# Separate buffers for the expert tables, and DMAs moved from SyncE's queue to ScalarE's and GpSimd's, in a two-layer attention, RWKV and PEER backbone

## The chip, the cores and the metric

The kernel runs on one core of a Trainium2 chip. The metric is the device time of one execution in microseconds, as a median over runs. The core's engines are TensorE (PE in the profile, with weight loads as PEld), VectorE (DVE), ScalarE (ACT), GpSimd (POOL) and SyncE (SP); SyncE computes nothing here and issues DMAs. Each engine works through its own instructions in a fixed order. A DMA is issued by one engine, in that order, and is then carried by the core's 16 DMA engines.

## The reference

Two layers work on 512 latent tokens and 256 context tokens of width 1024, in float32. Each layer has a mixer (windowed attention, 2-D neighbourhood attention and an RWKV-7 scan in parallel, one output projection) and then a PEER feed-forward part. The change touches PEER and the loads around it:

```python
def peer_ffn(h, wq, sub_keys, u, v):
    ...
        q = (hb @ wq).reshape(PEER_CHUNK, PEER_HEADS, 2, PEER_QDIM // 2)
        s = jnp.einsum('thpd,hpnd->thpn', q, sub_keys).astype(jnp.float32)
        sv, si = lax.top_k(s, PEER_TOPK)
    ...
        expert = i1 * PEER_NKEYS + i2
        gate = jax.nn.softmax(best, axis=-1)
        ue = jnp.take(u, expert, axis=0)
        ve = jnp.take(v, expert, axis=0)
        act = jax.nn.gelu(jnp.einsum('td,thkd->thk', hb, ue).astype(jnp.float32), approximate=False)
        return jnp.einsum('thk,thkd->td', (gate * act).astype(hb.dtype), ve)
```

Each token picks 16 of 16,384 experts in each of 8 heads, so 128 experts a token. An expert is one row of `u` (its score with the token goes through Gelu and is multiplied by the gate) and one row of `v` (which is added with that weight). In layer 0 all six tiles of 128 tokens pass through PEER; in layer 1 only the four latent ones are needed.

## The kernel before, in words

PEER is computed in two ways at once. Some token tiles are *dense*: four in layer 0, three in layer 1. For them TensorE multiplies the tokens with all 16,384 experts, and gates that are zero for experts not chosen pick out the right ones. The other tiles are *gathered*: the two context tiles in layer 0, one latent tile in layer 1. For them GpSimd issues indirect DMAs (`gather`, L1461) that fetch, for one of a token's 128 choices, the rows of `u` and `v` of 128 tokens: 128 rows of 8 KB, 1 MiB a gather. There are 256 gathers in layer 0 and 128 in layer 1. For each pair (`accumulate`) VectorE forms two dot products (L1472), ScalarE takes Gelu of both (L1474), VectorE multiplies by the gates (L1475) and adds the two `v` rows with these weights to `acc` (L1478).

A dense layer goes through its experts in 128 blocks of 128, four to a group, two to a table load of 1 MiB.

- Scores (`scored(g)`): a table `ur2` holds two blocks of `u` transposed (L1304). ScalarE rounds each to `uH` (L1311), VectorE takes the rest `uL` (L1313), and TensorE makes 24 matmuls into `pa` (three products, eight slices of the width), 512 columns wide in layer 0 and 384 in layer 1. ScalarE's Gelu gives `aw` (L1317), which is written to DRAM as `ascr` (L1319), or is kept in SBUF and multiplied by its gates at once. That is so for the last blocks: 32 in layer 0, 44 in layer 1. These read their gates back from DRAM as `wt`, one row buffer for a group (L1300): 8 reads in layer 0, 11 in layer 1. Hence 96 and 84 writes of `ascr`.
- Gates (`gates`): spread over the first groups (22 in layer 0, 18 in layer 1), one-hot matrices from VectorE and small matmuls into `pw` (L1233) make the gates of 32 tokens for all experts; ScalarE copies them to `W` (L1234, one buffer), and a 2 MiB DMA writes them to `wscr` (L1236): 16 writes in layer 0, 12 in layer 1.
- Values: with all scores done, a second loop loads tables of `v` (L1364), reads `ascr` and `wscr` back (L1357, L1359; none for kept blocks), rounds and splits (`vH`, `vL`, `GH`, `GL`), and accumulates in PSUM (`py`). Two blocks of layer 0 are 48 matmuls of 512 columns here too.

In layer 0's scores the modulation weights of layer 1 are also worked out: after every fifth group a `mod_unit` loads four row buffers of `w_mod` (L167), six units in all.

All these loads share one ring of row buffers (8 KB a partition): gathers, tables of both kinds, `wt`, `w_mod`, and, in the stages before, w_out, wq and residual rows. A buffer is given out in the order in which the program asks, so a request waits until the sixth request before it is done with:

```python
NROW = 6
NTICK = ((2, 1.2, 2.6, 1.75), (0, 0, 1.3, 0.9))
...
    def row(self):
        return self.gp.tile([P, 2 * D], F32, name="row", bufs=NROW)
```

How many gathers are asked for beside the dense work is set by `tick`. `NTICK[l][z]` is added to a count at each tick, and a gather is issued for each whole number. In layer 0: index 0, five ticks late in the latent `scores`; index 1, after every second block of the first 12 groups (24 ticks); index 2, the same in the other 20 groups (40 ticks); index 3, after every second block of the values (64 ticks). In layer 1 the first kind ends after 3 groups. What is left is gathered by `flush` after the values. Then `ends` and the lines after it multiply by the modulation, add the residual and write the result.

A scheduler fixes the order of the instructions on each engine when the program is built, by priorities and a simulated timeline; gathers and what belongs to them have a high priority. Before the change all the DMAs named here are in SyncE's queue, but for the gathers, which are in GpSimd's.

Of the kernel before, what the change touches and what calls it, by code (L numbers as in the profile page):

```python
# [18 lines left out]
P = 128  # L19
# [15 lines left out]
LATER = 2000  # L35
NROW = 6
NQ = 2
# [18 lines left out]

NTICK = ((2, 1.2, 2.6, 1.75), (0, 0, 1.3, 0.9))
NFIRST = (12, 3)
# [7 lines left out]
class Kernel:  # L66
# [82 lines left out]
    def mod_unit(self, l, ch, pool, ps, tag, row=None):  # L149
# [10 lines left out]
        for k in range(KC):  # L160
            if row is None:
                w = pool.tile([P, 1024], F32, name="wmod")
                nc.sync.dma_start(w, src[:, k])
            else:
                if k % 2 == 0:
                    w2 = row().rearrange("p (k n) -> p k n", k=2)
                    nc.sync.dma_start(w2, src[:, k:k + 2])  # L167
                w = w2[:, k % 2]
            for j in range(4):
                add(j, self.cs[:, k], w[:, j * 256:j * 256 + 256], k == 0, False)  # L170
# [1030 lines left out]
    def gates(self, t, pk, pool, ps):  # L1201
# [16 lines left out]
        for s_ in range(4):  # L1218
            W = pool.tile([P, P, 32], F32, name="W", bufs=1)
            for t4 in range(8):  # L1220
# [10 lines left out]
                for q in range(4):  # L1231
                    for z in range(2):
                        nc.tensor.matmul(pw[:, q], oh[:, 1, :, q], og[:, z, :, q], start=z == 0, stop=z == 1)  # L1233
                nc.scalar.activation(W[:, :, t4 * 4:t4 * 4 + 4], pw.rearrange("p q i -> p i q"), AF.Copy,  # L1234
                                     scale=1.0 / GSCALE)
            nc.sync.dma_start(self.wscr[:, 4 * t + s_], W)  # L1236
            yield
# [22 lines left out]
    def peer(self, l, st):  # L1260
# [11 lines left out]
        with ExitStack() as sb:  # L1272
# [23 lines left out]
            def scored(g, late=None):  # L1296

                if 4 * g >= P - nres - LATE[l]:
                    wt = gat.row()[:, :4 * nd].rearrange("p (a q t) -> p a q t", q=4, t=32)
                    nc.sync.dma_start(wt, self.wscr[:, :nd // 32, g * 4:g * 4 + 4, :])  # L1300
                for b in range(4 * g, 4 * g + 4):
                    if b % 2 == 0:
                        ur2 = gat.row().rearrange("p (z k n) -> p z k n", z=2, k=KC)
                        nc.sync.dma_start(ur2, i["uT"][l, b:b + 2].rearrange("z p k n -> p z k n"))  # L1304
# [13 lines left out]
                    if b not in keep:  # L1318
                        nc.sync.dma_start(self.ascr[g, :, b % 4, :nd], aw)  # L1319
                    else:  # L1320
# [26 lines left out]
        with ExitStack() as sb:  # L1347
# [5 lines left out]
            for g in list(range(n0, 32)) + list(range(n0)):  # L1353
# [6 lines left out]
                for q in range(4):  # L1360
                    b = g * 4 + q
                    if b % 2 == 0:
                        vr2 = gat.row().rearrange("p (z d) -> p z d", z=2)
                        nc.sync.dma_start(vr2, vtab[b * P:(b + 2) * P, :].rearrange("(z p) d -> p z d", p=P))  # L1364
# [64 lines left out]
class Gather:  # L1429
# [26 lines left out]
    def row(self):  # L1456
        return self.gp.tile([P, 2 * D], F32, name="row", bufs=NROW)

    def gather(self, a, k):
        r = self.row()  # L1460
# [6 lines left out]
    def accumulate(self, a, k):  # L1467
# [6 lines left out]
        nc.scalar.activation(dt, dt, AF.Gelu)  # L1474
        nc.vector.tensor_tensor(dt, dt, self.gate[:, a, k:k + NQ], OP.mult)  # L1475
        for z in range(NQ):
# [85 lines left out]
```

## Time and profile before

| what | value |
|---|---|
| median of 3 runs | 5024.15 us (5021.28 to 5025.62) |
| profiled execution, its own time | 5011.65 us |
| its span in the trace | 5009.9 us |
| TensorE busy | 4425.2 us, 88% of the span |
| VectorE busy | 3653.8 us, 73% |
| ScalarE busy | 1772.4 us, 35% |
| GpSimd busy | 1226.5 us, 24% |
| mean granted TensorE clock | 0.917 of full speed |
| bytes moved | 1186.55 MB, mean 237 GB/s |

The profile is one execution. An engine is busy while it runs an instruction; matmuls overlap, so TensorE's busy time doesn't say how fast it works, and the number of matmuls in a stretch is shown beside it. The granted clock is in parts of full speed (2.4 GHz; the lower level is 1.2 GHz), averaged over a stretch. The DMA share is the mean busy share of the 16 DMA engines.

### The profile page before, as it was taken

To read this page: it belongs to the slowest core of one execution; us is meant where nothing else is said; L and a number is where in the kernel's file an instruction comes from. 1 tells how busy PE (TensorE), PEld (TensorE's weight loads), DVE (VectorE), ACT (ScalarE), POOL (GpSimd) and SP (SyncE) were. 2 spreads that over 40 slices of the span, in tenths; PEclk is the share of its full clock that TensorE was granted. 3 is DMA by queue.
4 is the path that set the end of the run, shared out by engine and by line. 5 is a ranking of instruction groups with operands and counts; after the bars stand their busy time and mean duration, and the time that the engine had idled before them with its cause. 6 is when DMAs were issued, how large, how long until landed. Compare 5 with 4: busy or idle time off the path is not lost.

```text
span 5009.9 us, 74083 instructions
## 1 busy us (share of the span) xinstructions
PE 4425.2 (88%) x27525; PEld 3669.7 (73%) x27525; DVE 3653.8 (73%) x7587; ACT 1772.4 (35%) x2961; POOL 1226.5 (24%) x1347
## 2 busy tenths in 40 slices
PE   7778887789999988899999886799698997999999
PEld 4557776667787776677788664777588996988787
DVE  3974666889877876677788878557579875676776
ACT  3533245333333332222232354335334332333333
POOL 0025632151112222222222115354031110111120
PEclk9788797899999998999999987889899998999999
DMA  7444654255778888887999834573526885886897
GB/s 268 149 113 124 175 174 157 101 190 199 272 288 340 335 310 309 320 305 274 334 373 351 286 117 120 129 202 103 176 92 219 323 296 223 289 307 251 310 328 243
DMA packets 573481, 1186.55 MB, mean 237 GB/s; under 512 B 62768, under 2 KB 376000, under 8 KB 520384
## 3 DMA queue, kind: packets, MB, share of 16 engines
q1 hardware_dynamic: 506688, 758.39, 45.0%
q0 software_dynamic: 61440, 418.41, 22.6%
q10 hardware_dynamic: 4992, 5.02, 0.4%
q8 instruction: 216, 3.54, 0.3%
q14 instruction: 145, 1.19, 0.1%
HBM read 1005.19 MB, written 176.50 MB: 236 GB/s over the span
## 4 chain that ended last, share of the span: by engine, by line
PE 45%; DVE 16%; issue 15%; DMA 15%; POOL 4%; ACT 3%; SPq 1%; POOLq 0%; ACTq 0%; DVEq 0%
DMA row<-in_uv,eidx 6%; PE py L133 5%; PE py L132 4%; PE py L134 4%; PE pa L132 4%; PE pa L134 4%; PE pa L133 4%; PE pw L1233 3%; DMA row<-in_uT 3%; PE pf L132 2%; POOL row L1461 2%; PE pf L133 2%; PE pf L134 2%; DVE uL L1313 1%; PE pg L840 1%
## 5 line engine op out<-in xcount | busy, mean ns | idle before, releaser
L1461 POOL DMA_INDIRECT row<-in_uv,eidx x384 | 547.4, 1426 | 2350.1 <-DVE accc L1478 1153.0
L132 PE MATMUL pa<-hH,uH 128*128 128x512 f32 (+1 forms) x2048 | 772.8, 377 | 81.9 <-ACT uH L1311 68.0
L134 PE MATMUL pa<-hH,uL 128*128 128x512 f32 (+1 forms) x2048 | 764.6, 374 | 21.1 <-DVE uL L1313 21.0
L133 PE MATMUL pa<-hL,uH 128*128 128x512 f32 (+1 forms) x2048 | 762.8, 372 | 0.0
L133 PE MATMUL py<-vL,GH 128*128 128x512 f32 x1792 | 699.8, 392 | 19.8 <-DVE vL L1369 19.6
L134 PE MATMUL py<-vH,GL 128*128 128x512 f32 x1792 | 697.1, 391 | 0.0
L132 PE MATMUL py<-vH,GH 128*128 128x512 f32 x1792 | 684.3, 392 | 13.3 <-ACT vH L1367 9.2
L1472 DVE SCALAR_TENSOR_TENSOR row<-row,h2c 128x1024 f32<-128x1024 f32 x384 | 473.6, 1236 | 230.3 <-DMA row<-in_uv,eidx 229.8
L132 PEld LDWEIGHTS pa<-hH,uH 128*128 128x128 f32 x2048 | 399.5, 195 | 138.9 <-ACT uH L1311 79.0
L1478 DVE SCALAR_TENSOR_TENSOR accc<-row,dt,accc 128x1024 f32<-128x1024 f32 x384 | 494.2, 1287 | 5.7
L1311 ACT CAST uH<-row 128x1024 fp32r<-128x1024 f32 x256 | 266.2, 1049 | 570.1 <-PE pa L133 435.7
L134 PEld LDWEIGHTS pa<-hH,uL 128*128 128x128 f32 x2048 | 397.4, 194 | 74.6 <-DVE uL L1313 32.7
L1313 DVE TENSOR_TENSOR uL<-row,uH 128x1024 fp32r<-128x1024 f32 x256 | 311.6, 1222 | 161.4 <-ACT uH L1311 156.4
L133 PEld LDWEIGHTS pa<-hL,uH 128*128 128x128 f32 x2048 | 398.8, 195 | 40.1
L133 PEld LDWEIGHTS py<-vL,GH 128*128 128x128 f32 x1792 | 338.6, 189 | 97.2 <-DVE vL L1369 26.9
L132 PEld LDWEIGHTS py<-vH,GH 128*128 128x128 f32 x1792 | 339.2, 189 | 86.0 <-ACT vH L1367 10.0
L134 PEld LDWEIGHTS py<-vH,GL 128*128 128x128 f32 x1792 | 338.8, 189 | 70.0
L1369 DVE TENSOR_TENSOR vL<-row,vH 128x1024 fp32r<-128x1024 f32 x256 | 311.5, 1220 | 13.4 <-ACT vH L1367 13.1
L1367 ACT CAST vH<-row 128x1024 fp32r<-128x1024 f32 x256 | 266.4, 1044 | 15.5 <-DMA row<-in_uv 13.5
L1225 DVE TENSOR_TENSOR oh<-iota,ix 128x512 f16<-128x512 f16 x448 | 171.9, 421 | 135.5 <-PE pw L1233 135.1
L1233 PE MATMUL pw<-og,oh 128*128 128x128 f16 x1792 | 237.9, 297 | 36.4 <-DVE og L1228 19.2
L1233 PEld LDWEIGHTS <-oh 128*128 128x128 f16 x1792 | 190.4, 119 | 76.6 <-DVE og L1228 35.1
(380 smaller groups left out, 8352.1 us busy)
## 6 DMA issues: line engine op xcount, KB each, us to landing
row<-in_uT SPq DMA_DIRECT2D x128, 1024.0 KB
row<-in_uv SPq DMA_DIRECT2D x128, 1024.0 KB
wscr<-W SPq DMA_DIRECT2D x28, 2048.0 KB
wmod<-in_w_mod SPq DMA_DIRECT2D x48, 512.0 KB
row<-in_wq SPq DMA_DIRECT2D x24, 1024.0 KB
ascr<-aw SPq DMA_DIRECT2D x96, 256.0 KB
row<-in_w_mod SPq DMA_DIRECT2D x24, 1024.0 KB
av<-ascr SPq DMA_DIRECT2D x48, 512.0 KB
```

Of the source, the lines that this page charges most:

```text
L132: mm(out, lh, rh, start=first, stop=False)
L133: mm(out, lh, rl, start=False, stop=False)
L134: mm(out, ll, rh, start=False, stop=last)
L1225: nc.vector.tensor_tensor(oh[:, z], self.iota4, ix[:, z, tt].unsqueeze(1).to_broadcast([P, P, 4]), OP.is_equal)
L1233: nc.tensor.matmul(pw[:, q], oh[:, 1, :, q], og[:, z, :, q], start=z == 0, stop=z == 1)
L1311: nc.scalar.copy(uH, ur)
L1313: nc.vector.tensor_tensor(uL, ur, uH.bitcast(F32), OP.subtract)
L1367: nc.scalar.copy(vH, vr)
L1369: nc.vector.tensor_tensor(vL, vr, vH.bitcast(F32), OP.subtract)
L1461: self.K.nc.gpsimd.indirect_dma_start(out=r, out_offset=None, in_=self.K.i[f"uv{self.l}"], in_offset=bass.IndirectOffsetOnAxis(ap=self.idx ...
L1472: nc.vector.scalar_tensor_tensor(rows[z][:, 0:D], rows[z][:, 0:D], 1.0, self.h[:, a], OP.mult, OP.mult, accum_out=dt[:, z:z + 1])
L1478: nc.vector.scalar_tensor_tensor(acc, v, dt[:, z:z + 1], acc, OP.mult, OP.add)
```

## The change

- The tables of scores and values get a ring of their own of two buffers (`table`, `NTAB`); four are left for everything else.
- The writes of `ascr` and `wscr` are issued by ScalarE, the reads of `wt` and the loads of `w_mod` by GpSimd, in place of SyncE.
- In `accumulate`, the two products with the gates become two ScalarE operations with the gate as scale, in place of one on VectorE.
- The gather rates change: in layer 0 from 2.6 to 2.3 in the later scores and from 1.75 to 1.9 in the values, in layer 1 from 1.3 to 1.2 and from 0.9 to 1.0.

```diff
-NROW = 6
+NROW = 4
+NTAB = 2
...
-NTICK = ((2, 1.2, 2.6, 1.75), (0, 0, 1.3, 0.9))
+NTICK = ((2, 1.2, 2.3, 1.9), (0, 0, 1.2, 1.0))
...
                     w2 = row().rearrange("p (k n) -> p k n", k=2)
-                    nc.sync.dma_start(w2, src[:, k:k + 2])
+                    nc.gpsimd.dma_start(w2, src[:, k:k + 2])
...
-            nc.sync.dma_start(self.wscr[:, 4 * t + s_], W)
+            nc.scalar.dma_start(self.wscr[:, 4 * t + s_], W)
...
                     wt = gat.row()[:, :4 * nd].rearrange("p (a q t) -> p a q t", q=4, t=32)
-                    nc.sync.dma_start(wt, self.wscr[:, :nd // 32, g * 4:g * 4 + 4, :])
+                    nc.gpsimd.dma_start(wt, self.wscr[:, :nd // 32, g * 4:g * 4 + 4, :])
...
-                        ur2 = gat.row().rearrange("p (z k n) -> p z k n", z=2, k=KC)
+                        ur2 = gat.table().rearrange("p (z k n) -> p z k n", z=2, k=KC)
...
-                        nc.sync.dma_start(self.ascr[g, :, b % 4, :nd], aw)
+                        nc.scalar.dma_start(self.ascr[g, :, b % 4, :nd], aw)
...
-                        vr2 = gat.row().rearrange("p (z d) -> p z d", z=2)
+                        vr2 = gat.table().rearrange("p (z d) -> p z d", z=2)
...
+    def table(self):
+        return self.gp.tile([P, 2 * D], F32, name="tab", bufs=NTAB)
+
...
-        nc.vector.tensor_tensor(dt, dt, self.gate[:, a, k:k + NQ], OP.mult)
+        for z in range(NQ):
+            nc.scalar.activation(dt[:, z:z + 1], dt[:, z:z + 1], AF.Copy, scale=self.gate[:, a, k + z:k + z + 1])
```

## Rows read from the trace of the kernel before

**Rows 1.** Busy us (instructions) per engine in stretches, granted clock, DMA share, GB/s

```profile
1400.00:1500.00 100.00, 100.00 (x573) 81.40 (x572) 73.49 (x127) 34.24 (x57) 16.18 (x14) 1.00 0.82 311
...
1600.00:1700.00 100.00, 95.88 (x481) 78.13 (x479) 78.76 (x128) 31.66 (x55) 22.93 (x16) 0.95 0.89 341
...
1700.00:2140.00 440.00, 372.39 (x1829) 293.21 (x1830) 309.69 (x453) 116.28 (x189) 101.97 (x71) 0.92 0.87 319
...
2500.00:2600.00 100.00, 100.00 (x443) 82.80 (x442) 86.12 (x114) 29.78 (x45) 22.79 (x17) 1.00 1.01 376
...
4080.00:4460.00 380.00, 333.04 (x1910) 319.31 (x1909) 251.67 (x378) 121.28 (x195) 53.30 (x42) 0.91 0.74 270
4460.00:4860.00 400.00, 390.19 (x1709) 320.34 (x1708) 291.48 (x400) 144.22 (x216) 63.25 (x43) 1.00 0.85 298
```

**Rows 2.** TensorE's matmuls of tile `pa` alone, in stretches

```profile
1400.00:1500.00 100.00, 77.88 (x328) 1.00 0.82 311
1700.00:2140.00 440.00, 307.49 (x1248) 0.92 0.87 319
...
4080.00:4460.00 380.00, 295.56 (x1571) 0.91 0.74 270
4300.00:4400.00 100.00, 94.46 (x521) 0.97 0.81 298
```

**Rows 3.** TensorE's waits, 1700 to 2140 us: total us, times, longest

```profile
PE pa L132 <- ACT uH L1311: 40.7, 10, 11.7
PE pm L159 <- DMA row<-in_w_mod: 10.7, 5, 4.6
```

**Rows 4.** Timeline of ScalarE, 1895 to 1960 us

```profile
1926.76 1.99 ACT L1311 CAST uH<-row 128x1024 fp32r<-128x1024 f32 x2 [11.30 <-DMA row<-in_uT]
```

**Rows 5.** TensorE's waits, 4080 to 4460 us

```profile
PE pa L132 <- ACT uH L1311: 26.0, 5, 15.4
PE pw L1233 <- ACT W L1234: 8.1, 2, 7.0
...
PE pa L132 <- ACT aw L1317: 3.2, 2, 2.8
```

**Rows 6.** TensorE's waits, 3700 to 4080 us

```profile
PE pa L132 <- ACT aw L1317: 8.5, 7, 2.8
```

**Rows 7.** TensorE's waits, 2140 to 2400 us

```profile
PE py L132 <- ACT vH L1367: 9.2, 2, 6.7
```

**Rows 8.** SyncE's queue: waits, 1700 to 2140 us

```profile
SPq L1319 <- ACT aw L1317: 76.8, 17, 15.8
SPq L1304 <- DVE accc L1478: 55.4, 8, 12.0
```

**Rows 9.** Timeline of SyncE's queue, 1895 to 1960 us

```profile
1897.94 7.72 SPq L167 DMA_DIRECT2D row<-in_w_mod  x4
1906.61 0.55 SPq L1300 DMA_DIRECT2D row<-wscr  x1
1907.68 11.61 SPq L1304 DMA_DIRECT2D row<-in_uT  x2
```

**Rows 10.** VectorE's waits over the whole span

```profile
DVE row L1472 <- DMA row<-in_uv,eidx: 229.8, 91, 7.9
```

**Rows 11.** Instructions of L1319: ns min/median/max, first and last start

```profile
L1319 SPq DMA_DIRECT2D ascr<-aw x180: 319/320/1259, 1151.2 to 4213.0; - x180
```

**Rows 12.** Instructions of L502, a plain DMA in GpSimd's queue

```profile
L502 POOL DMA_DIRECT2D tscr<-tt x32: 764/772/817, 301.4 to 3244.8; - x32
```

**Rows 13.** Instructions of L1461, the gathers

```profile
L1461 POOL DMA_INDIRECT row<-in_uv,eidx x384: 932/1214/4301, 1017.6 to 4921.8; - x192
```

**Rows 14.** Groups by line: busy us, mean ns of one, idle before

```profile
L1474 ACT ACTIVATE dt<-dt 128x2 f32<-128x2 f32 x192 | 38.8, 202 | 479.2 <-DVE row L1472 479.0
...
L1475 DVE TENSOR_TENSOR dt<-dt,gatec 128x2 f32<-128x2 f32 x192 | 29.8, 155 | 15.0 <-ACT dt L1474 15.0
```

**Rows 15.** Timeline of VectorE at the end of layer 0, 2815 to 2880 us

```profile
2851.36 1.28 DVE L1478 SCALAR_TENSOR_TENSOR accc<-row,dt,accc 128x1024 f32<-128x1024 f32 x1
```

## The prediction

> **What bounds the kernel now.** I read the busy time by stretch first. The PEER part of layer 0 runs from about 1,150 to 2,870 us, that of layer 1 from about 3,560 us to the end; each is a stretch of scores (uT tables, matmul tile `pa`) and then one of values (uv tables, tile `py`). TensorE stands out in all of them, so the question is how much of each stretch it loses. Its pitch at full rate is seen in [rows 1]: in the values of layer 0, 443 matmuls filled 100 us, 0.2257 us each. In the scores, `pa` is mixed with gate matmuls [rows 1, 2]: of 573 matmuls in a fully busy 100 us, 328 are `pa`, 328 x 0.2257 = 74.0 us, which leaves 26 us for 245 others, 0.106 us each. The narrower `pa` of layer 1 took 94.46 / 521 = 0.181 us [rows 2].
>
> Now the two scoring stretches that fall behind. In 1700 to 2140 us TensorE issued 1829 matmuls, 1248 of them `pa` [rows 1, 2]: 1248 x 0.2257 + 581 x 0.106 = 343 us of work in 440 us, 97 us lost. Of these 440 - 372.4 = 67.6 us were idle; the other 29 us are matmuls at the lower of the clock's two levels (granted 0.92 there against 1.00 in the full slices), which follows the pauses. In 4080 to 4460 us it is 1571 x 0.181 + 339 x 0.106 = 321 us in 380 us: 59 lost, 47 idle, 12 slow. The values of layer 1 are at 390.2 of 400 us busy, and those of layer 0 reach 100 of 100: little is to be had there.
>
> What ended the idle time says which part is the tables' [rows 3 to 7]: in the first stretch 40.7 of 67.6 us are `uH`, ScalarE's rounding of a table, and ScalarE itself was waiting for the table to land (11.30 us in [rows 4]); 10.7 us are a w_mod row. In the second 26.0 us are `uH`, 8.1 us `W` and 3.2 us `aw`, the two tiles whose writes SyncE issues. Between 3700 and 4080 us `aw` costs another 8.5 us, and in 2140 to 2400 us a late value table 9.2 us.
>
> Why the tables are late stands in SyncE's own queue [rows 8, 9]. It waited 76.8 us at L1319 for an activation to write, and 55.4 us at L1304 for a gather's accumulation to free a shared buffer. Before the 11.30 us pause, four w_mod loads and a gate read went first, and only then the two tables, whose issues took 11.61 us together and which landed 19 us after 1907.68.
>
> **The change part by part.** *Own buffers for tables.* A table now waits only for the table two before it. A period is two blocks, 48 `pa` matmuls or 10.8 us at full rate; the old ring of six served one table, 2.6 gathers and about half a row of other loads in it, so it went round in 6 / 4.1 = 1.5 periods, and the tables' wait hung on gathers. Two periods, 21.7 us, stand against the 19 us landing that hurt. Gathers keep their depth: 4 / (2.3 + 0.5) = 1.4 periods in place of 1.5. In layer 0 the 40.7 us of idle time bring their share of slow clock, 40.7 / 67.6 x 97 = 58 us. The bytes limit this: 319 GB/s over 440 us are 140.4 MB; the 26 periods move 26 x 0.3 = 7.8 gathers of 1.05 MB away, which leaves 132.2 MB, 388 us at the 341 GB/s of [rows 1] (52 us gained) or 352 us at its 376 GB/s (88 us). From below, at the present 319 GB/s, 414 us: 26 gained. I take 40, three quarters of 52, since VectorE still waits for gathers in its own order (229.8 us over the run, [rows 10]) and a table is rounded there too.
>
> *Writes on ScalarE's queue.* 180 `ascr` and 28 `wscr` writes leave SyncE, which keeps almost nothing but tables while scoring. An issue took 0.320 us, at most 1.259 [rows 11]: 208 x 0.32 = 67 us of ScalarE's time, in stretches where it is about 30% busy (116.3 of 440 us). What waits behind one is the next rounding; the write's own wait is short, since ScalarE made the data just before. Cost 0, bound 10 us. A write held like the 11.61 us pair would hold a rounding, but in 180 none was held over 1.3 us. The return in layer 1, with `uH`, is (26.0 + 8.1 + 3.2) / 47 x 59 = 47 us; I take three quarters, 35, and 6 of the 8.5 us before it. Bytes don't limit here (270 GB/s).
>
> The Trainium skill says in "DMA: Bandwidth & Descriptors", under "Issuing engines are not separate DMA queues", that DMAs started by several engines run on the same 16 DMA engines, so that spreading them saves only the issuing time. By that rule the moved writes give nothing: a rival below. The trace speaks against it only so far as one queue's order makes a ready load wait behind an unready write: 76.8 us in [rows 8].
>
> *w_mod and gate reads on GpSimd's queue.* 24 w_mod loads (6 units of four) and 19 gate reads, 43 issues. A plain GpSimd issue took 0.77 us, a gather's 1.21 (up to 4.30) [rows 12, 13]: 33 to 52 us on an engine busy for 102 of the 440 us of the first stretch. Behind a waiting one stand the gathers, behind them VectorE. One w_mod unit takes all four row buffers. Both ends: nothing, as the gathers have 1.4 periods, or 7.9 us, the longest gather wait, for each of 6 units and 19 reads, 198 us. The mean of those waits is 229.8 / 91 = 2.5 us; I take 0 in the sum, as a ring of about equal depth leaves gathers where they were, and keep the other end as a rival.
>
> *Gate product on ScalarE.* Out go 192 VectorE products of 0.155 us, 30 us; in come 384 ScalarE ops. Nearest is the Gelu of the same tile, 0.202 us [rows 14]: 78 us. VectorE then waits some 0.3 us longer per pair, unless other work stands between. Neither engine is full. Cost 0, bounds -10 and +15.
>
> *New gather rates.* Layer 0: 40 ticks at 2.3 for 2.6 while scoring, 64 at 1.9 for 1.75 in the values: -12 and +9.6. Before, 254 of 256 gathers went out on ticks; now 252, and one more pair is flushed after the last tick. The last accumulation already ends the stage [rows 15]; four VectorE passes of some 1.25 us, 5 us more. In the values 1 table, 1.9 gathers and 1 MiB of reads a period are 4.09 MB, at 376 GB/s 10.88 us against TensorE's 10.84: 2 us in 48 periods (at 351 GB/s it would be 39). Against that stands 7 of the 9.2 us of the late value table. I put the values at 0, -7 to +32.
>
> *Four rows instead of six elsewhere.* w_out, wq and residual rows have less prefetch: 5 us, bounds 0 and 15, the trace showing no such wait.
>
> Sum: -40 - 35 - 6 + 0 + 5 + 5 = -71 us. The profiled execution took 5011.65 us (span 5009.9), 12.5 under the median of the runs: 5011.65 - 71 = 4941, so 4953 us by the runs' median, 1.4% less. A measurement tells about 0.2%, 10 us, from no change.
>
> **The rivals.** *All the lost time returns*: the pauses end altogether, and with them the slow clock. 97 + 59 + 8 - 10 = 154 us, 4870. For it: TensorE reaches 100 of 100 us where the tables are on time. Against: 132.2 MB then need 385 GB/s, more than any slice shows.
>
> *Moved queues are worth nothing* (the page's rule): `W` and `aw` stay late. The sum loses 11 us (three quarters of 11.3 / 47 x 59) and the 6: -54, 4970.
>
> *The wait passes from tables to gathers*: each engine's order is fixed at build time, and VectorE stands at a late gather with `uL` behind it. For it: those waits are 229.8 us today. A third more, 76 us, ends at 5024 or just above: no change.
>
> *GpSimd's queue makes it slower*: a gate read or a w_mod load waits at its head for a row, and gathers behind it come too late for VectorE's order. 25 such places at 5 us are 125 us: -71 + 125 = +54, 5078. It decides from 71 / 25 = 2.8 us a place, just above today's mean of 2.5. For it: the ring of four is filled by one w_mod unit. Against: the same loads took ring places before.
>
> The Trainium skill's "SBUF — State Buffer", under "SBUF: two separate sides", warns that descriptors of a GpSimd DMA can't be written while VectorE holds the shared port, and advises the queues of ScalarE or SyncE. The spread of the gather's issue, 0.93 to 4.30 us, agrees in direction; no run here separates it.
>
> **How the numbers follow.** The forecast, 4885 to 5000 around 4953, gets 0.48; all returned 0.14; queues worth nothing 0.08; passed to gathers 0.12; slower by GpSimd's queue 0.18. So faster 0.70, same 0.12, slower 0.18. The range 4860 to 5050 leaves out some 0.06 below and 0.13 above.
>
> **What would show it.** Right: the 40.7 and 26.0 us of `uH` fall to a third, granted clock in the two stretches above 0.95, scoring of layer 0 some 40 us shorter, the values unchanged. Wrong: VectorE's wait for gathers well over 230 us, GpSimd standing at L167 or L1300, or ScalarE standing at a write.

## The result, and the profile after

The changed kernel takes 4965.82 us (median of 4 runs, 4963.13 to 4971.35); the kernel before took 5022.72 us beside it (4 runs, 5010.22 to 5025.62). The ratio is 0.9893, 95% interval 0.9874 to 0.9912: 57 us or 1.1% faster. The forecast was 4953 us, 12.8 us below the result. The two profiled executions, 5011.65 and 4964.34 us, differ by 47.3, and the account below is made with them. So the time is close to the forecast; the parts that make it up are not, as the rest shows.

Lines of the changed kernel: score tables are loaded at L1305, rounded to `uH` at L1312; `aw` comes from L1318 and is written at L1320; `W` comes from L1235; gates are read at L1301; value tables are loaded at L1365 and rounded to `vH` at L1368; gathers are L1465, their dot products L1476, the gate product L1480, the accumulation L1483. The matmuls of `pa` and `py` are at L133 to L135.

Five landmarks on TensorE cut the run into stages. These are the rows of its matmuls by tile, for the kernel before (nanoseconds, then first and last start in us); the third is the value stage of layer 0 alone.

```profile
L134 PE MATMUL pa<-hH,uL x2048: 333/389/796, 1104.8 to 4463.7; 128*128 128x512 f32 x94, 128*128 128x384 f32 x93
L134 PE MATMUL py<-vH,GL x1792: 387/389/628, 2128.0 to 5001.5; 128*128 128x512 f32 x200
L132 PE MATMUL py<-vH,GH x1024: 387/389/795, 2124.2 to 2851.6; 128*128 128x512 f32 x171
L132 PE MATMUL py<-WH,oH x128: 389/393/794, 950.6 to 3608.3; 128*128 128x512 f32 x128
```

The same rows of the changed kernel:

```profile
L135 PE MATMUL pa<-hH,uL x2048: 331/389/687, 1020.0 to 4388.5; 128*128 128x512 f32 x94, 128*128 128x384 f32 x93
L135 PE MATMUL py<-vH,GL x1792: 387/389/628, 2054.8 to 4954.1; 128*128 128x512 f32 x200
L133 PE MATMUL py<-vH,GH x1024: 388/389/794, 2049.6 to 2781.5; 128*128 128x512 f32 x171
L133 PE MATMUL py<-WH,oH x128: 387/393/796, 932.5 to 3547.6; 128*128 128x512 f32 x128
```

Taking differences of these starts gives the time of each stage, in us:

| stage | before | after | difference |
|---|---|---|---|
| start to first value matmul of layer 0 | 2124.2 | 2049.6 | -74.6 |
| values of layer 0 | 727.4 | 731.9 | +4.5 |
| from there to the end of layer 1's output projection (left-over gathers, mixer) | 756.7 | 766.1 | +9.4 |
| scores of layer 1, to the last `pa` | 855.4 | 840.9 | -14.5 |
| values of layer 1, to the last `py` | 537.8 | 565.6 | +27.8 |
| all | 5001.5 | 4954.1 | -47.4 |

Two things are seen at once. The gain ahead of layer 0's values is nearly twice the 40 us forecast, and that of layer 1's scores about a third of the 41. And 28 us are lost again in a stage for which the forecast had nothing. How far a stage differs between kernels that share its code is seen below; layer 1's scores are the one where this matters.

TensorE's waits of the changed kernel over the whole span (total us, times, longest) no longer have a line for `uH`, which answers to [rows 3, 5]; what heads them is a value table, where [rows 7] had 9.2 us:

```profile
PE py L133 <- ACT vH L1368: 41.8, 26, 3.8
...
PE pa L133 <- ACT aw L1318: 22.7, 16, 2.6
PE pw L1234 <- ACT W L1235: 22.6, 8, 5.3
...
PE pa L133 <- ACT ar L1318: 15.2, 2, 7.7
```

From VectorE's waits over the span, which answer to [rows 10]: the wait for gathers has fallen from 229.8 to 73.0 us. (The longest is now that of `GL` for ScalarE's `GH`, 210.5 us, where it was 78.7.) The second line, a wait for gates read back, has no counterpart in the kernel before; it is taken up below.

```profile
...
DVE row L1476 <- DMA row<-in_uv,eidx: 73.0, 40, 7.1
DVE ar L1323 <- DMA row<-wscr: 59.6, 6, 23.3
```

The two scoring stretches that were read before in [rows 1], up to their ends (columns as there), and then TensorE's `pa` alone in them:

```profile
1700.00:2050.00 350.00, 309.63 (x1571) 248.74 (x1570) 233.48 (x335) 111.49 (x210) 81.87 (x62) 0.92 0.84 305
3960.00:4389.00 429.00, 391.11 (x2350) 377.00 (x2348) 278.78 (x423) 155.26 (x269) 63.13 (x46) 0.94 0.70 251
```

```profile
1700.00:2050.00 350.00, 262.08 (x1099) 0.92 0.84 305
3960.00:4389.00 429.00, 332.16 (x1816) 0.94 0.70 251
```

By the prediction's pitches the work in them is 1099 x 0.2257 + 472 x 0.106 = 298 us of 350, and 1816 x 0.181 + 534 x 0.106 = 385 of 429. So 52 and 44 us are still lost, where it was 97 of 440 and 59 of 380, and the granted clock is 0.92 and 0.94, not above 0.95. What ended the idle time that is left is spread over many things: in the first stretch 11.5 us for the first `GH` of the values, 7.7 for `ar`, 7.6 for `W` and 5.5 for a w_mod row; in the second 11.1 us for `W`, 9.4 for `uL` (VectorE's part of a table) and 7.5 for `ar`.

### The profile page after: what moved, and what is told of

Read it like the earlier page. It is cut to its first block, busy times and chain, and to the rows that moved or that the text cites. A ratio compares the mean times of both kernels' runs of the same rounds, so it can differ in the third digit from the quotient of the medians.

```text
span 4962.6 us, 73858 instructions
## 1 busy us (share of the span) xinstructions
PE 4429.9 (89%) x27525; PEld 3668.8 (74%) x27525; DVE 3635.2 (73%) x7395; ACT 1867.3 (38%) x3347; POOL 1330.2 (27%) x1390
## 5 line engine op out<-in xcount | busy, mean ns | idle before, releaser
L1465 POOL DMA_INDIRECT row<-in_uv,eidx x384 | 599.4, 1561 | 1570.5 <-DVE accc L1483 1150.1
L133 PE MATMUL pa<-hH,uH 128*128 128x512 f32 (+1 forms) x2048 | 760.5, 371 | 38.1 <-ACT aw L1318 22.7
L135 PE MATMUL pa<-hH,uL 128*128 128x512 f32 (+1 forms) x2048 | 758.6, 371 | 20.4 <-DVE uL L1314 20.3
L134 PE MATMUL py<-vL,GH 128*128 128x512 f32 x1792 | 699.8, 392 | 13.0 <-DVE vL L1370 12.8
L135 PE MATMUL py<-vH,GL 128*128 128x512 f32 x1792 | 696.0, 390 | 0.0
L133 PE MATMUL py<-vH,GH 128*128 128x512 f32 x1792 | 587.1, 393 | 55.2 <-ACT vH L1368 41.8
L1476 DVE SCALAR_TENSOR_TENSOR row<-row,h2c 128x1024 f32<-128x1024 f32 x384 | 471.9, 1234 | 74.5 <-DMA row<-in_uv,eidx 73.0
L1483 DVE SCALAR_TENSOR_TENSOR accc<-row,dt,accc 128x1024 f32<-128x1024 f32 x384 | 497.8, 1296 | 36.3 <-ACT dt L1480 28.8
L1312 ACT CAST uH<-tab 128x1024 fp32r<-128x1024 f32 x256 | 268.7, 1051 | 653.4 <-PE pa L134 608.8
L133 PEld LDWEIGHTS pa<-hH,uH 128*128 128x128 f32 x2048 | 393.1, 192 | 88.7 <-ACT aw L1318 29.1
L135 PEld LDWEIGHTS pa<-hH,uL 128*128 128x128 f32 x2048 | 392.3, 192 | 73.7 <-DVE uL L1314 29.2
L133 PEld LDWEIGHTS py<-vH,GH 128*128 128x128 f32 x1792 | 335.7, 189 | 136.6 <-ACT vH L1368 53.4
L1314 DVE TENSOR_TENSOR uL<-tab,uH 128x1024 fp32r<-128x1024 f32 x256 | 318.3, 1244 | 138.1 <-ACT uH L1312 137.7
L135 PEld LDWEIGHTS py<-vH,GL 128*128 128x128 f32 x1792 | 337.2, 188 | 69.6
L1370 DVE TENSOR_TENSOR vL<-tab,vH 128x1024 fp32r<-128x1024 f32 x256 | 308.8, 1220 | 17.3 <-ACT vH L1368 17.1
L1379 ACT CAST GH<-G 128x512 fp32r<-128x512 f32 (+1 forms) x180 | 102.9, 572 | 520.1 <-PE py L134 366.7
L1368 ACT CAST vH<-tab 128x1024 fp32r<-128x1024 f32 x256 | 261.1, 1044 | 21.4 <-DMA tab<-in_uv 21.3
```

What stands on the lines that cost most here:

```text
L133: mm(out, lh, rh, start=first, stop=False)
L134: mm(out, lh, rl, start=False, stop=False)
L135: mm(out, ll, rh, start=False, stop=last)
L1312: nc.scalar.copy(uH, ur)
L1314: nc.vector.tensor_tensor(uL, ur, uH.bitcast(F32), OP.subtract)
L1368: nc.scalar.copy(vH, vr)
```

## The experiments

Twelve more kernels were run. Ratios are to the kernel before, timed beside each. Where a stage is given, it is worked out from the same five landmarks of that kernel's profiled execution. Executions of one kernel differ by up to some 30 us (those with three value tables lay between 4947.35 and 4977.56), so a few us in one stage of one profile say little, and ratios with overlapping intervals aren't told apart.

| kernel | ratio, 95% interval | first value matmul | values of layer 0 | scores of layer 1 | values of layer 1 |
|---|---|---|---|---|---|
| before | 1 | 2124.2 | 727.4 | 855.4 | 537.8 |
| only the table ring | 0.9900, 0.9884 to 0.9915 | 2077.5 | 734.9 | 830.7 | 561.5 |
| only the four queue moves | 0.9908, 0.9893 to 0.9923 | 2106.6 | 721.8 | 841.1 | 547.3 |
| only the writes moved | 0.9988, 0.9978 to 0.9999 | 2121.9 | 720.8 | 854.7 | 538.9 |
| the change | 0.9893, 0.9874 to 0.9912 | 2049.6 | 731.9 | 840.9 | 565.6 |
| change, gate reads on SyncE | 0.9861, 0.9841 to 0.9880 | 2058.3 | 735.7 | 828.5 | 569.9 |
| change, gate reads and w_mod on SyncE | 0.9874, 0.9854 to 0.9893 | 2050.7 | 732.8 | 825.4 | 567.0 |
| change, gate product on VectorE | 0.9905, 0.9888 to 0.9923 | 2060.6 | 740.0 | 824.3 | 570.7 |
| change, old gather rates | 0.9883, 0.9866 to 0.9900 | 2082.2 | 733.2 | 837.5 | 563.9 |
| change, three value tables | 0.9897, 0.9877 to 0.9917 | 2060.1 | 697.5 | 826.9 | 556.6 |
| change, half the value tables in the row ring | 1.0031, 1.0019 to 1.0043 | 2057.4 | 815.8 | 826.3 | 561.6 |
| the same, old gather rates | 1.0026, 1.0017 to 1.0035 | 2074.3 | 785.4 | 842.4 | 565.0 |
| half of all tables in the row ring, gate reads on SyncE | 1.0332, 1.0312 to 1.0352 | 2161.1 | 785.6 | 889.7 | 570.7 |
| change, gate reads on SyncE, earlier gathers | 0.9895, 0.9879 to 0.9912 | 2067.6 | 736.7 | 834.0 | 560.9 |

**Only the table ring.** The kernel before with this alone:

```diff
-NROW = 6
+NROW = 4
+NTAB = 2
...
-                        ur2 = gat.row().rearrange(
+                        ur2 = gat.table().rearrange(
...
-                        vr2 = gat.row().rearrange(
+                        vr2 = gat.table().rearrange(
...
+    def table(self):
+        return self.gp.tile([P, 2 * D], F32, name="tab", bufs=NTAB)
```

> The kernel before with nothing but the rings split (four row buffers, two for tables); queues, gate product and rates as before. If the scores gain because a table no longer waits for gathers, this alone gives most of it: about 4970 us (before 5022.7, changed 4965.8), with TensorE's wait for uH falling from 68 us over the run to under 25. If the order of SyncE's queue was the cause (tables behind writes and w_mod loads), it gives little: 5005 to 5025 us, and uH still waits above 45 us.

Measured: 4971.11 us, 0.9900. The ring alone has, within what can be told, the whole effect of the change: the gain in both scores and the loss in layer 1's values (561.5 us). It is also what cut the gather wait of VectorE (59.9 us). In layer 1, between 3570 and 4400 us, these are waits of SyncE's queue in this kernel, the first of them those at the writes of `aw`:

```profile
SPq L1320 <- ACT aw L1318: 244.2, 64, 12.0
SPq L1305 <- DVE uL L1314: 195.2, 40, 14.2
SPq L1237 <- ACT W L1235: 66.5, 11, 14.8
```

SyncE still stands for 244 us at unready writes, and yet TensorE waits for no `uH`. With a ring of two, loaded ahead, the queue has the time to stand there.

**Only the queues.** The kernel before with the four DMA moves:

```diff
-                    nc.sync.dma_start(w2, src[:, k:k + 2])
+                    nc.gpsimd.dma_start(w2, src[:, k:k + 2])
...
-            nc.sync.dma_start(self.wscr[:, 4 * t + s_], W)
+            nc.scalar.dma_start(self.wscr[:, 4 * t + s_], W)
...
-                    nc.sync.dma_start(wt, self.wscr[:, :nd // 32, g * 4:g * 4 + 4, :])
+                    nc.gpsimd.dma_start(wt, self.wscr[:, :nd // 32, g * 4:g * 4 + 4, :])
...
-                        nc.sync.dma_start(self.ascr[g, :, b % 4, :nd], aw)
+                        nc.scalar.dma_start(self.ascr[g, :, b % 4, :nd], aw)
```

> The kernel before with nothing but the four DMAs moved to the queues of ScalarE and GpSimd; one ring of six, gate product on VectorE, old rates. If the order of SyncE's queue was the cause: about 4970 to 4985 us. If the shared ring was: 5005 to 5025 us. If a gate read on GpSimd's queue holds the gathers whatever the rings are, GpSimd shows a wait at the gate read for a write of the gates of 100 us or more, and it may be slower than before, up to 5040 us.

Measured: 4976.07 us, 0.9908. So 48 and 43 us, each alone, against 57 together. The parts don't add up: both shorten the same wait for `uH`. But the queues leave half of it in place (68.0 us over the span before). GpSimd's stands at a gate read for gates being written are 83.0 us here, under the 100 of the third expectation, and the kernel is not slower.

```profile
PE pa L132 <- ACT uH L1311: 34.1, 20, 7.9
```

**Only the writes.** Which of the four moves counts? The second and the fourth alone, in the kernel before:

> The kernel before with only the writes of ascr and wscr moved to ScalarE's queue. Theory A, a ready table load stood behind an unready write in SyncE's queue: this alone carries most of what the four moved queues gave together (0.9908), 0.989 to 0.994, and TensorE's wait for uH falls from 68 us to about 35. Theory B, the w_mod loads and gate reads ahead of the tables held them: 0.997 to 1.002, uH above 55 us.

Measured: 5007.92 us, 0.9988, the interval just below 1. The theory that a table stood behind an unready write falls. TensorE's wait, over the span:

```profile
PE pa L132 <- ACT uH L1311: 66.6, 18, 15.7
```

SyncE's queue in this kernel, 1700 to 2140 us, shows why. The 76.8 us at the write of [rows 8] are gone, and yet all its waits together are 399 us of these 440, where they were 381 before: the queue stands at the next things in its order instead. The longest waits are for a shared buffer that a gather or a w_mod row still holds (55.4, 37.9, 18.4 and 17.5 us before):

```profile
SPq L1304 <- DVE accc L1478: 68.1, 8, 16.0
SPq L1300 <- DVE accc L1478: 36.9, 5, 15.8
SPq L1304 <- DVE dt L1475: 28.1, 3, 12.2
SPq L1304 <- PE pm L159: 25.4, 3, 11.5
```

So, by difference, nearly all of what the four moves gave together comes with moving the w_mod loads and gate reads, which no longer go ahead of the tables. A kernel with those two moves alone was not run; that the writes count once the others are away is not ruled out.

**Gate reads back on SyncE.** In the changed kernel GpSimd's queue has two long stands at a gate read, 243.5 us, besides many short ones at gate reads and w_mod loads that wait for a row buffer. From its waits over the span:

```profile
...
POOL row L1301 <- DMA wscr<-W: 243.5, 2, 196.4
...
POOL row L1301 <- DVE accc L1483: 70.3, 11, 11.6
...
POOL row L168 <- DVE accc L1483: 63.7, 14, 15.5
```

The longest stand in its timeline (start, duration, line; in brackets the idle time before and what ended it):

```profile
3999.90 1.68 POOL L1465 DMA_INDIRECT row<-in_uv,eidx  x1 [8.10 <-DVE accc L1483]
4198.00 1.11 POOL L1301 DMA_DIRECT2D row<-wscr  x1 [196.42 <-DMA wscr<-W]
```

For 196 us no gather is issued, since the gate read ahead of them wants gates that are still being written. The experiment takes this stand away:

```diff
-                    nc.gpsimd.dma_start(wt, self.wscr[:, :nd // 32, g * 4:g * 4 + 4, :])
+                    nc.sync.dma_start(wt, self.wscr[:, :nd // 32, g * 4:g * 4 + 4, :])
```

> The changed kernel with the gate reads alone back on SyncE's queue. In the changed kernel GpSimd stood 196 us at one gate read in layer 1 (and 47 us at one in layer 0) with all gathers behind it, and they were made up in the values of layer 1, where TensorE fell to 85 to 93 us per 100. If that is what the values of layer 1 lost: about 4940 us (28 us in the values of layer 1 come back). If the values are held by bytes or by ScalarE's order whatever came before: 4960 to 4970 us. If the same early gate read now holds tables on SyncE's queue: 4980 us or more.

Measured: 4953.98 us, 0.9861, the lowest ratio of all, its interval overlapping that of the change by a hair: 0.0032 lower, some 16 us, and not certain. The scores of layer 1 are 828.5 us for 840.9, but this can't be put down to the stand: with three value tables, 241.6 us were waited at the same line, and the stage took 826.9. The values of layer 1 aren't shorter: gathers there still come at 22 to 23 per 100 us. So a stand of 196 us cost little or nothing: those 16 us hold all that the gate reads cost on GpSimd's queue.

**Gate reads and w_mod loads back on SyncE.** Also the first of the four moves undone:

> The changed kernel with gate reads and w_mod loads both back in SyncE's queue, so that GpSimd issues gathers alone. Theory A, waits at the head of GpSimd's queue still cost (gate reads back gave 0.9861 against 0.9893): 0.980 to 0.986, with more gathers issued between 1400 and 1900 us than the 49 of the changed kernel. Theory B, the ring of four holds the gathers, whichever queue issues the w_mod loads, and the tables stand behind the four w_mod loads again: 0.987 to 0.994, gathers between 1400 and 1900 us still 45 to 52.

Measured: 4943.06 us, 0.9874. Not told apart from the last. Between 1400 and 1900 us GpSimd issued 49 gathers, as many as in the changed kernel: the ring of four holds them, whichever queue loads w_mod. Given the ring of tables, no gain is seen from moving w_mod and gate reads.

**Gate product back on VectorE.**

```diff
-        for z in range(NQ):
-            nc.scalar.activation(dt[:, z:z + 1], dt[:, z:z + 1], AF.Copy, scale=self.gate[:, a, k + z:k + z + 1])
+        nc.vector.tensor_tensor(dt, dt, self.gate[:, a, k:k + NQ], OP.mult)
```

> The changed kernel with the product with the gates back on VectorE as one operation. If the three small operations in ScalarE's order make the roundings of value tables late (TensorE waited 41.8 us for vH in the changed kernel, 9.2 before): 4945 to 4955 us, and that wait falls under 20 us. If the product costs nothing where it is, as predicted: 4960 to 4972 us.

Measured: 4972.29 us, 0.9905: no difference from 0.9893 that can be told, and TensorE's wait for `vH` stays (44.7 us).

**The old gather rates.** The changed kernel with the rates of before:

```diff
-NTICK = ((2, 1.2, 2.3, 1.9), (0, 0, 1.2, 1.0))
+NTICK = ((2, 1.2, 2.6, 1.75), (0, 0, 1.3, 0.9))
```

> The changed kernel with the gather rates of before (2.6 and 1.75 in layer 0, 1.3 and 0.9 in layer 1). Theory A, the bytes hold layer 0's values: a period of two blocks there moves 3.93 MB in place of 4.09, 11.1 us for 11.55 at the 354 GB/s of the changed kernel, so the value stretch of layer 0 falls from 740 to 715 us or less and TensorE is at 100 of 100 us and 443 matmuls in more slices; the 12 gathers that go back into the scores cost 0 to 37 us there. The whole: 0.984 to 0.992 of the kernel before, against 0.989 for the changed one. Theory B, the two-buffer ring holds the values whatever the bytes: the stretch stays at 730 to 745 us with 400 to 410 matmuls per 100 us, and the whole rises by the later scores, 0.990 to 0.996.

Measured: 4958.21 us, 0.9883, as the changed kernel. Of the two theories the ring of two holds: the values of layer 0 stay at 733.2 us. For the whole, that theory's 0.990 to 0.996 was too high. The first value matmul starts 33 us later (2082.2), as 12 more gathers lie ahead of it; but the stretch from layer 0's last value matmul to layer 1's output projection is 749.5 us in place of 766.1. The rates mostly shift work.

**Three value tables.** A third buffer in the values, from another pool (room for it comes from `yt`, which in layer 0 shares the buffer of `G`):

```diff
-                        vr2 = gat.table().rearrange(
+                        vr2 = (gat.table() if b // 2 % 3 < 2 else vp.tile([P, 2 * D], F32, name="vt", bufs=1)).rearrange(
...
```

> The changed kernel with a third buffer for value tables alone, in a pool of the values (the last tiles of layer 0 share another tile's buffers to make room); the gathers' ring is untouched. If two table buffers are too few, TensorE's wait for vH (41.8 us) falls under 15 and the time to 4925 to 4940 us. If the gathers' lost pace is the cause, the DMA engines stay at 0.97 while gathers last and the time stays at 4950 to 4970 us.

Measured: 4963.14 us, 0.9897: no change. But the stage changes completely. The windows of this kernel in layer 0's values, and after them:

```profile
2100.00:2700.00 600.00, 600.00 (x2648) 496.84 (x2648) 494.77 (x618) 206.97 (x374) 156.15 (x104) 1.00 0.97 347
2700.00:2800.00 100.00, 58.46 (x258) 48.05 (x257) 77.00 (x97) 20.78 (x53) 30.78 (x23) 0.82 0.79 287
```

TensorE is busy for 600 of 600 us, and the wait for `vH` is gone. The stage takes 697.5 us, 34 less. All of it is given back next (808.0 us to layer 1's output projection, in place of 766.1), where TensorE waits once for the left-over gathers of the context tiles, 14 of them, to be accumulated and normalised:

```profile
PE pt L215 <- DVE xn L209: 71.7, 1, 71.7
```

With two tables TensorE paused a little in every period while the gathers went on; with three it doesn't, and the gathers come that much later.

**Half the value tables in the row ring.** The three next kernels try to get back a pace that the shared ring had kept. In the values of layer 1 before, gathers were spread evenly. GpSimd's gathers (busy us and number, then granted clock, DMA share, GB/s) in the kernel before:

```profile
4500.00:4600.00 100.00, 17.37 (x13) 1.00 0.71 255
4600.00:4700.00 100.00, 11.35 (x11) 1.00 0.80 281
4700.00:4800.00 100.00, 16.98 (x10) 0.98 0.94 325
```

and in the changed kernel:

```profile
4400.00:4500.00 100.00, 33.78 (x22) 1.00 0.97 357
4500.00:4600.00 100.00, 34.81 (x22) 1.00 0.97 356
4600.00:4700.00 100.00, 17.93 (x12) 0.97 0.98 359
4700.00:4800.00 100.00, 0.00 (x0) 1.00 0.73 225
```

All engines in three of these stretches of the changed kernel:

```profile
4500.00:4600.00 100.00, 92.72 (x400) 73.91 (x399) 92.49 (x115) 39.81 (x76) 34.81 (x22) 1.00 0.97 356
4600.00:4700.00 100.00, 85.56 (x358) 68.01 (x357) 82.17 (x108) 34.11 (x64) 17.93 (x12) 0.97 0.98 359
4700.00:4800.00 100.00, 100.00 (x443) 82.81 (x442) 54.71 (x74) 35.89 (x50) 0.00 (x0) 1.00 0.73 225
```

While gathers come at 22 per 100 us the DMA share is 0.97, VectorE is at 92 of 100, and TensorE loses; when they are done it fills the slice. A likely reason is that the shared ring had let a gather go only as tables were used. The experiment:

```diff
-                        vr2 = gat.table().rearrange(
+                        vr2 = (gat.row() if b // 2 % 2 else gat.table()).rearrange(
```

> The changed kernel, but every second value table comes from the row ring of four again. New theory: with a ring of its own nothing but the ring holds the gathers to the pace of the ticks; in the values of layer 1 they ran at 22 per 100 us in place of 11 to 13, the DMA engines were at 0.97, and TensorE waited. Tables in the gathers' ring pace them again: 11 to 13 gathers per 100 us to the end of layer 1, its values in about 535 us (566 in the changed kernel), those of layer 0 in about 722 (740): 4915 to 4930 us. Rival, that two table buffers are too few: the same direction, since tables also get deeper, but the gathers' pace stays. Rival, that GpSimd's early gate read did it: 4960 to 4970 us.

Measured: 5031.0 us, 1.0031, slower than before. The pace did come back (14, 11, 12 and 12 gathers per 100 us from 4500 to 4900 us), but layer 0's values take 815.8 us, since SyncE again waits at a value table for a gather's buffer (from its waits, 2060 to 2880 us), and TensorE waits 83.0 us in all for `vH`:

```profile
...
SPq L1365 <- DVE accc L1483: 200.7, 27, 17.2
...
SPq L1365 <- DMA row<-in_uv,eidx: 62.8, 11, 14.0
```

**The same with the old rates**, as in the diff above:

> As values_mixed, with the old gather rates (2.6 and 1.75 in layer 0, 1.3 and 0.9 in layer 1). If the rates matter little once the ring paces the gathers: within 8 us of values_mixed. If 1.9 a period is too much for the values of layer 0 (349 GB/s over the stage, DMA engines at 0.96): 8 to 20 us faster than values_mixed.

Measured: 5027.65 us, 1.0026. So the rates don't explain that this kernel is slow. They move time within it: layer 0's values take 785.4 us in place of 815.8, but they start 17 us later, and layer 1's scores take 16 us more.

**Half of all tables in the row ring**, those of the scores too, with gate reads on SyncE:

> Every second table of the scores and of the values from the row ring, and the gate reads on SyncE's queue; the writes stay on ScalarE's, w_mod on GpSimd's. If pace is what counts everywhere and the early gate read costs too: the best so far, 4900 to 4925 us. If tables in the scores need their own buffers to be on time, uH waits for tables again (over 30 us) and it is 4940 us or more.

Measured: 5176.41 us, 1.0332, and TensorE waits 139.7 us for `uH` again. The more tables stand among gathers in a ring of four, the slower: what the change gained by separating them is shown once more from the other side.

**Earlier gathers.** Gate reads on SyncE, and

```diff
-NTICK = ((2, 1.2, 2.3, 1.9), (0, 0, 1.2, 1.0))
+NTICK = ((2, 1.4, 2.5, 1.65), (0, 0, 1.3, 0.9))
```

> Gate reads back in SyncE's queue as in the run with 0.9861, and the gathers of layer 0 issued earlier: rates 1.4, 2.5 and 1.65 in place of 1.2, 2.3 and 1.9, layer 1 at 1.3 and 0.9. Theory A, the bytes of layer 0's values hold TensorE there, and the slices from 1000 to 1900 us have room (DMA share 0.49 to 0.87): values of layer 0 back at 443 matmuls per 100 us, 25 to 40 us shorter, scores at most 15 longer: 0.979 to 0.985. Theory B, gathers come no earlier, as the ring of four and VectorE's order hold them, and TensorE waits in the scores in place of the values: 0.986 to 0.993.

Measured: 4957.09 us, 0.9895. Nothing gained by the rates, so the theory that bytes hold layer 0's values falls, and the windows of this kernel say it more sharply:

```profile
2400.00:2700.00 300.00, 281.36 (x1209) 224.55 (x1208) 245.51 (x304) 96.86 (x180) 80.78 (x51) 1.00 0.98 354
2700.00:2800.00 100.00, 95.71 (x417) 77.67 (x416) 64.99 (x77) 27.69 (x44) 9.85 (x6) 1.00 0.68 244
```

In the last slice the gathers are over and the DMA share is 0.68, and still TensorE makes 417 matmuls of 443. With three tables it made 443 at a share of 0.97. Two buffers hold it, not bytes: 48 matmuls at 1209 in 300 us are 11.9 us for a table, 23.8 for the round trip of two, against 21.7 at TensorE's pitch. The timelines of this kernel show the same round trip, and what it is made of. SyncE's queue, with two loads into one buffer (one into the other buffer lies between them):

```profile
2726.62 0.38 SPq L1365 DMA_DIRECT2D tab<-in_uv  x1
...
2750.40 0.37 SPq L1365 DMA_DIRECT2D tab<-in_uv  x1
```

ScalarE, which rounds the first of these tables at 2744.58 us:

```profile
2743.43 0.62 ACT L1379 CAST GH<-G 128x512 fp32r<-128x512 f32 x1 [4.94 <-PE py L134]
...
2744.58 1.98 ACT L1368 CAST vH<-tab 128x1024 fp32r<-128x1024 f32 x2
```

ScalarE does not wait for the table: it waits for TensorE, at the `GH` that stands ahead in its order. By the times of the loads' semaphores in the trace, a table had landed 9.4 us after its issue (median of the 25 loads between 2400 and 2700 us) and then lay for 9.0 us until ScalarE came to it; some 5 us later VectorE had read it too, and the next load was issued. So the transfer itself is under half of the round trip.

## Why the prediction was right, and where it was not

*What bounds the kernel, and why tables are late* was right in its main part. Late score tables cost TensorE 68 us of waits, and the ring of two ends them. Of SyncE's two waits in [rows 8], ending the one for a shared buffer was enough (the ring alone, 0.9900). The one at unready writes was not the cause: taken away alone, it gave 0.9988, and left alone under the ring it did no harm. The prediction weighed waits of a queue as if the longest were the dearest. The shared buffer isn't the only remedy, though: with one ring of six, the four moves together halved the wait for `uH` and gave 0.9908.

*Own buffers for tables*: -40 was mis-sized. Up to the first value matmul the change gained 74.6 us, the ring alone 46.7 (2077.5). The step looked for it in the stretch from 1700 us on, which begins with the 1824th `pa`. From there to the last `pa` the change takes 386 us in place of 418: 32 gained, not far from the 40. But at that 1824th `pa` it was already 59 us ahead (1644.5 for 1703.2), and ahead of the stretch the prediction had booked nothing. A small part is that tables with a ring of their own are loaded ahead: the first `pa` starts at 1019 us in place of 1098, of which 22 us are left when the first table's 48 matmuls have started (1130.2 for 1152.6). And after the last `pa` some 16 us are lost again, as is told below under the gate reads. The lower gather rate takes gathers out of the scores: with the old rates the gain to the first value matmul is 42.0 (2082.2), so the rates are up to 33 of the 75; by the other kernels with the ring and either pair of rates (2050.7 to 2060.6, and 2074.3) it can be as little as 14. The bytes' limit at 341 GB/s was not reached: 305 were moved from 1700 to 2050 us.

*Writes on ScalarE's queue*: -35 and -6 failed. This is the largest wrong step. The scores of layer 1 are 854.7 us with only the writes moved, 855.4 before. The ring gives that stage's gain by itself: 830.7 us with it alone, 25 less. The four moves alone give 14 (841.1), by difference not through the writes. The change itself has 840.9 in its profile, but three kernels with the same ring and the same queues in that stage (three value tables, half the value tables in the row ring, gate product on VectorE) have 824 to 827, so the stage gained 14 to 31 us, not 41, and none of it is shown to come from the writes. ScalarE's cost was sized rightly at nothing: an issue there took 0.326 us in the median, at most 0.837, with no wait to speak of:

```profile
L1320 ACTq DMA_DIRECT2D ascr<-aw x180: 321/326/837, 1040.2 to 4145.5; - x180
```

The rival *moved queues are worth nothing* (4970) gave the better account of the sum than the forecast did: the ring without any moved queue is at 0.9900, the change at 0.9893. The Trainium skill's rule of "DMA: Bandwidth & Descriptors", "Issuing engines are not separate DMA queues", agrees with the writes (0.9988). It doesn't cover the four moves together while tables still share the ring (0.9908): there, by difference, the order of one queue mattered, for loads that went ahead of the tables.

*Values at 0, -7 to +32*: layer 0's values are at +4.5, rightly sized, but for another reason than the bytes that were worked out. The 9.2 us of a late first table went, and a small pause in each period came. The prediction set two periods of 21.7 us against a landing of 19 us. Here a table landed in 9.4 us; what the prediction left out is that it lies until ScalarE's order comes to it, and that its buffer is free only when the second engine has read it. The round trip is 23.8 us. Layer 1's values, which the forecast passed over as nearly full, lost 27.8 us. It comes with the ring (561.5 with the ring alone, 547.3 with the queues alone). Bunched gathers are seen with it wherever the value tables have the ring to themselves. That they are the whole cause isn't shown: three tables, other rates and the shared ring all left 557 to 565 us there, the shared ring with a pace that was even but with waits of its own.

*Gate reads and w_mod on GpSimd*: GpSimd did stand at L168 and L1301, one of the signs that the prediction gave for being wrong. The rival's 25 places at 5 us are nearly what is seen: 25 waits for a gather's accumulation to free a row, 134 us, and two more, 196 and 47 us, for gates still being written, which the prediction did not name. The price of the gate reads' share is between nothing and the 16 us of the two ratios, at the low end of the bounds of 0 and 198. So the rival that had the change slower had the right places and lengths and a price far too high; VectorE's wait for gathers, which should have grown, fell.

One such place does cost time, and it comes with the split of the rings. From the last `pa` of layer 0 to the first value matmul the change takes 19.0 us. It is 2.5 us in the four kernels whose score tables, all or every second, come from the row ring, and 12.6 to 35.1 in those with a table ring for all of them. The kernels with one ring of six have no wait of VectorE for gates read back; all others do. GpSimd's queue, with the last w_mod load of a unit that fills the ring of four, and the gate read behind it:

```profile
2024.52 0.71 POOL L168 DMA_DIRECT2D row<-in_w_mod  x1 [5.55 <-PE pm L160]
2031.81 1.17 POOL L1301 DMA_DIRECT2D row<-wscr  x1 [6.58 <-DMA row<-in_w_mod]
```

and VectorE, which needs these gates for the last scores before it goes on:

```profile
2043.15 2.50 DVE L1323 TENSOR_TENSOR ar<-ar,row 128x512 f32<-128x512 f32 x4 [23.28 <-DMA row<-wscr]
```

It isn't the queue: with gate reads on SyncE the gap is 14.2 us, with w_mod loads there too 12.6.

*Gate product*: 0 was right. One operation took 0.283 us in place of the 0.202 taken from the Gelu beside it, so ScalarE does 109 us in place of 78, unseen in the time.

```profile
L1480 ACT ACTIVATE dt<-dt,gatec x384: 277/283/298, 1032.7 to 4671.5; 128x1 f32<-128x1 f32 x192
```

*New rates* +5 and *fewer rows elsewhere* +5: the stretch behind layer 0's values grew by 9.4 us. With the old rates and the smaller ring it is 749.5, shorter than the 756.7 before, so no price of the smaller ring is seen there (the 16 us above lie elsewhere); with the earliest gathers it is 736.4. The sum of the rates isn't told from zero (0.9883 against 0.9893).

*The other rivals.* All lost time returns: no, in the two stretches 96 of 779 us are still lost, where it was 156 of 820. The wait passes to gathers: no, that wait fell by 157 us.

Up to layer 1's output projection -40 + 5 + 5 = -30 us were forecast and -60.7 measured; from there on -41 and +13.3. The errors, -31 and +54, cancel to 24 us between the profiled executions (-71 and -47), and to 13 between forecast and median. The time was right with two steps wrong: that it came out so close is luck in good part.

The change is not the best of these kernels: with gate reads left on SyncE it is at 0.9861, with w_mod too at 0.9874. Their intervals overlap that of the change, so that some 10 to 16 us are likely and not certain. Three value tables together with gathers moved to earlier wasn't tried; the two profiles suggest that each removes what the other runs into.

## What to carry to other kernels

A queue that issues in order can stand nearly all the time, as SyncE's did here (381 of 440 us before, 399 with the writes gone): the time at one wait is not its price, since with that wait gone the queue stands at the next. Ask which of its waits would still be there without the others, and test by moving one alone. Giving a prefetched stream a ring of its own ends its waits for other streams, but also the pace that the shared ring had set; look then at the stage after it for bunched transfers, and compare the round trip of a buffer (load, landing, the turn of every reader in its engine's order) with the number of buffers times the period. Where the smaller ring that is left is filled by one group of loads, ask what is issued behind them, and who needs it first. And where two engines share a stage's work, freeing the one lets the other's left-over come due at the stage's end.

## What was not expected of the hardware

With the DMA engines nearly full, at shares of 0.97 to 0.98, the stretches shown here moved 347 GB/s over 600 us, 354 over 300 and 356 to 359 in slices of 100; the single slice of [rows 1] with 376 is no rate to plan a stage by. A gather's issue on GpSimd took 1.67 us in the median after the change, 1.21 before [rows 13]; in both kernels the shortest is 0.93 us. It comes with the ring: 1.68 us with the ring alone, 1.21 with the queues alone, 1.22 with the writes alone; why, no run shows. With the ring alone:

```profile
L1465 POOL DMA_INDIRECT row<-in_uv,eidx x384: 932/1676/4017, 1003.7 to 4645.9; - x192
```

And 196 us without a single gather issued, in a stage where GpSimd issues all of them, cost little: the two kernels with and without that stand differ by some 16 us, which is not certain.
